# An encoder layer on one core: combinations made in two parts, first weights in a place of their own, v's transposes and the first scores moved back

## The chip, the cores and the metric

The kernel runs on one core of a Trainium2 chip. The metric is the device time of one execution in microseconds (us). The engines are named as the profile names them: PE (TensorE, the matrix engine; PEld are its weight loads), DVE (VectorE), ACT (ScalarE), POOL (GpSimd) and SP (SyncE, which here only issues DMAs). A granted clock of 1.00 means TensorE at full speed.

## The reference

One inference step of a single encoder layer over 576 rows: 512 rows of a new stream (the prompt) and 64 rows of a running stream (the sample), which brings states and 256 past keys and values.

```python
h = layer_norm(ALPHA * x + 0.5 * swiglu_ffn(x, p['ffn1_w_gu'], p['ffn1_w_down']), p['ln1_g'], p['ln1_b'])
mix, new_state = token_mixer(h, p, conv_prev, ml_state, att_past)
h = layer_norm(ALPHA * h + mix, p['ln2_g'], p['ln2_b'])
h = layer_norm(ALPHA * h + 0.5 * swiglu_ffn(h, p['ffn2_w_gu'], p['ffn2_w_down']), p['ln3_g'], p['ln3_b'])
```

```python
def token_mixer(xn, p, conv_prev, ml_state, att_past):
    (ml_q, ml_k, ml_v, ml_o, ml_i, ml_f, a_q, a_k, a_v, g_ml, g_att) = jnp.split(xn @ p['w_in'], SPLIT_IDX, axis=-1)
    ...
    qk = jax.nn.silu(causal_dwconv(qk_pad, p['ml_conv_w'], p['ml_conv_b']))
    ...
    h_ml, (C1, n1, m1) = mlstm_run(qm, km, vm, li, lf, (C0.astype(f32), n0.astype(f32), m0.astype(f32)))
    ...
    y_att = o.reshape(b, t, ATT_WIDTH) @ p['w_att_proj']
    merged = jax.nn.sigmoid(g_ml) * y_ml + jax.nn.sigmoid(g_att) * y_att
    return merged @ p['w_out'], new_state
```

The width is 1024, the FFN's 2816; the mLSTM has 4 heads of 256, the attention 16 heads of 64 with a bias by distance and a causal band in chunks of 64 rows. The sample rows attend to 256 past and 64 new rows. Everything is float32.

## The kernel before

**Arithmetic.** Activations lie transposed, 128 features by 576 rows, in 8 tiles. Each operand of a large product is split into a rounded part ("hi", a cast by ACT) and the rest ("lo", a subtraction by DVE, or by ACT and an accumulating DMA of POOL's queue in `add_lo`). One product is three matmuls: hi·hi, hi·lo, lo·hi (`mm3`, and the inner part of `gemm`). A column tile is 128 output features; its 576 rows go through PE as two halves, in two PSUM banks.

**Order.** PE's order is written out by the program. Class `Order` keeps a virtual clock, `od.now`, to which each matmul adds its estimated nanoseconds; `later(dt, fn)` puts a task into PE's stream once `dt` units have gone by. All the other engines are ordered by a scheduler, by priority (`hot(n)` raises it) and by when an instruction could start; `tc.issue_after(x)` forces an instruction behind x. DMA queues run in the order of their issues: one that waits for its place holds the ones behind it. PSUM has two tags of four banks, "mm" and "aux".

**Weights.** `pump` loads column weights in a fixed plan (`wr`, two buffers), casts and splits them into `wh` and `wl` (NWB = 4 slots). Keys in EARLY and EARLY1 are loaded and split in places of their own (`eh`, `el`) by `early`, long before use; keys in ADDED take their lo part by `add_lo`.

**Pairs.** FFN gate and up columns, and the mLSTM's v and o columns, are made in pairs by a scheme with seven products in place of eight: class `Units` (`prep` parts "a", "s", "t", "u", "b" make the weights' combinations in `ws` and `wt` and split them; `load` brings a pair's raw weights, `wu`, through SP) and class `Combos`. `Combos.add` makes eight sums of activations, `Combos.make` casts and splits them: for t2 and t4 first, then for t1 and t3, all in one go on ACT.

**Stages.** FFN1: first columns by `gemm` (three with WAVE3), then pairs, then the down projection and LN1. Mixer: v, k, q of the first attention pair of heads and the mLSTM gates by one `gemm` in WAVE_M order (so 4 column groups share the PSUM banks), then two v columns from EARLY1, then pairs of v and o columns, whose results go to DRAM (VD, OD). Then eight attention stages `att_qkv(j)`, `att_core(j)`, each for two heads: the transposes of v (`v_tr`), the split and doubled keys kh and kl (`dup`, on POOL, ACT and DVE), the bias tile G with a masked corner written by POOL at the end, and scores (`score`, `score_s`), whose result leaves its bank by a DVE instruction that adds G. The first pair's columns were made in the mixer's first gemm, so in its stage the next pair's columns are the only products around. Then four mLSTM heads: `ml_kq(h)` makes two k and two q columns with their convolutions on DVE and ACT and transposes k (`turn5`); `ml_early(h)` transposes v, whose tiles were loaded from VD in `ml_kq`. Then projections, LN2, and FFN2: four columns by `gemm` in WAVE4 order, whose weights lie in EARLY, then pairs; LN3.

**Places touched.** `Combos.make` and its callers; `Units.load` and the pools `sw` and `cw` for raw weights and sums, `sx` and `cx` for the rest; EARLY and ADDED; `values_s`, which multiplies the sample rows' probabilities (psh, psl) by values vc, where hi and lo of a head stand side by side as 128 columns, so that one matmul makes both, and the halves are added by ACT and DVE afterwards; the start time `t` of the scores in `att_core`; `ml_kq` and `ml_early`.

## Time and profile before

| | us |
|---|---|
| median of 3 runs | 1604.13 (1602.84 to 1610.17) |
| the profiled execution | 1607.91 |
| its span | 1606.1 |
| PE busy | 1576.4 |
| DVE busy | 1051.4 |
| ACT busy | 897.6 |
| POOL busy | 188.0 |

The granted clock over the whole span is 0.994. The span runs from the first to the last instruction. Busy times are summed over an engine's instructions and don't count waits; a row of the list of waits gives the line and tile of the instruction that waited, then what released it, then the total wait, how often, and the longest. Rows of a timeline give the start, the length, the engine, the line, the result's and the operands' names and shapes, and in brackets how long the engine had been idle before it and what ended that.

### The profile page before, as it was taken

Reading aid. Unit: us, or ns where it says so; the run is one execution under the profiler, and the core shown is the slowest. Engines: PE = TensorE matmul, PEld = TensorE weight load, DVE = VectorE, ACT = ScalarE, POOL = GpSimd, SP = SyncE. Lnnn points to the kernel's source line nnn. Section 1 sums busy time; section 2 is a strip of 40 time slices with the busy share of each in tenths; the row PEclk is TensorE's granted clock in tenths of the full one; section 3 lists DMA queues with packets and bytes.
Section 4 is the critical chain, followed back from the end, with each engine's and each line's share of the span. In section 5 each row is a group of like instructions: output and inputs, shape, how many; then the busy total and the mean of one; then the engine's idle time right before and its main releaser. Section 6 shows DMA issues by size and latency. Waiting matters only on the chain. (4 is left out here: it accounts for less than half of the span.)

```text
span 1606.1 us, 29438 instructions
## 1 busy us (share of the span) xinstructions
PE 1576.4 (98%) x11719; PEld 1554.9 (97%) x11719; DVE 1051.4 (65%) x2143; ACT 897.6 (56%) x1624; POOL 188.0 (12%) x349
## 2 busy tenths in 40 slices
PE   9999999999899899999999999999999999999998
PEld 8999999999899899999999999999999999999997
DVE  7777777627756667767623677755677777776636
ACT  7554555324845767767754887683446454555223
POOL 2000000000200432432111121101111000000000
PEclk9999999999999999999999999999999999999999
DMA  9222222224833666666788556533445222213333
GB/s 266 91 105 80 105 80 73 83 86 156 189 125 126 169 147 156 151 148 139 182 200 207 138 125 142 119 101 131 128 109 138 79 106 80 105 54 96 112 90 125
DMA packets 71970, 202.36 MB, mean 126 GB/s; under 512 B 7960, under 2 KB 17816, under 8 KB 71832
## 3 DMA queue, kind: packets, MB, share of 16 engines
q1 hardware_dynamic: 58584, 159.31, 30.3%
q0 software_dynamic: 12672, 40.64, 15.3%
q8 instruction: 92, 1.51, 0.4%
q10 hardware_dynamic: 576, 0.52, 0.1%
q14 instruction: 46, 0.38, 0.1%
HBM read 177.05 MB, written 16.32 MB: 120 GB/s over the span
## 5 line engine op out<-in xcount | busy, mean ns | idle before, releaser
L128 PE MATMUL mm<-s,wh 128*128 128x288 f32 (+2 forms) x3574 | 732.6, 299 | 0.2 <-ACT s L427 0.2
L128 PEld LDWEIGHTS mm<-s,wh 128*128 128x128 f32 x3574 | 576.3, 190 | 3.7 <-issue 0.6
L128 PE MATMUL mm<-s,wl 128*128 128x288 f32 (+2 forms) x1771 | 524.9, 296 | 0.7 <-DVE wl L145 0.7
L128 PEld LDWEIGHTS mm<-s,wl 128*128 128x128 f32 x1771 | 335.8, 190 | 1.0 <-DVE wl L145 1.0
L142 ACT ACTIVATE wh<-wr 128x1024 fp32r<-128x1024 f32 (+2 forms) x147 | 148.1, 1009 | 247.1 <-PE mm L128 224.5
L145 DVE TENSOR_TENSOR wl<-wr,wh 128x1024 fp32r<-128x1024 f32 (+2 forms) x88 | 101.4, 1155 | 102.4 <-ACT wh L142 102.3
L145 DVE TENSOR_TENSOR wl<-ws,wh 128x1024 fp32r<-128x1024 f32 x46 | 56.4, 1225 | 122.3 <-ACT wh L142 122.0
L128 PE MATMUL mm<-h,wh 128*128 128x256 f32 (+1 forms) x672 | 134.7, 294 | 0.0
L142 ACT ACTIVATE wh<-ws 128x1024 fp32r<-128x1024 f32 x46 | 48.8, 1061 | 108.9 <-PE mm L128 107.5
L128 PEld LDWEIGHTS mm<-h,wh 128*128 128x128 f32 x672 | 107.6, 188 | 0.2
L128 PE MATMUL mm<-tx,wh 128*128 128x288 f32 x522 | 106.9, 296 | 0.0
L128 PE MATMUL mm<-h,wl 128*128 128x256 f32 (+1 forms) x336 | 98.7, 294 | 0.0
L450 POOL TENSOR_TENSOR rs<-var,mhalf 128x2 f32<-128x2 f32 (+1 forms) x6 | 5.2, 860 | 737.5 <-DVE var L148 737.5
L128 PEld LDWEIGHTS mm<-tx,wh 128*128 128x128 f32 x522 | 83.4, 188 | 0.0
L182 POOL DMA_DIRECT2D wl<-in_w_in x50 | 45.0, 900 | 280.7 <-ACT wl L142 246.7
L128 PE MATMUL mm<-tx,wl 128*128 128x288 f32 x261 | 76.9, 295 | 0.0
L128 PE MATMUL mm<-tx,ah 128*128 128x288 f32 x344 | 72.2, 302 | 0.1
L142 ACT ACTIVATE wh<-wu 128x1024 fp32r<-128x1024 f32 x46 | 48.9, 1063 | 32.1 <-PE mm L128 31.3
L128 PEld LDWEIGHTS mm<-h,wl 128*128 128x128 f32 x336 | 63.0, 188 | 0.0
L142 ACT ACTIVATE wl<-wh 128x1024 fp32r<-128x1024 f32 x58 | 61.2, 1055 | 0.5
L145 DVE TENSOR_TENSOR ws<-wu 128x1024 f32<-128x1024 f32 x46 | 56.0, 1218 | 7.1 <-DMA wu<-in_w_gu 6.9
L145 DVE TENSOR_TENSOR wl<-wt,wh 128x1024 fp32r<-128x1024 f32 x46 | 56.0, 1218 | 6.5 <-ACT wh L142 6.5
(339 smaller groups left out, 3499.5 us busy)
## 6 DMA issues: line engine op xcount, KB each, us to landing
wu<-in_w_gu SPq DMA_DIRECT2D x78, 512.0 KB, 4.3
wr<-in_w_in SPq DMA_DIRECT2D x58, 512.0 KB, 4.6
wl<-in_w_in POOLq DMA_DIRECT2D x50, 512.0 KB, 5.7
wr<-in_w_dn SPq DMA_DIRECT2D x40, 512.0 KB, 3.6
wr<-in_w_dn SPq DMA_DIRECT2D x20, 384.0 KB, 3.2
wu<-in_w_in SPq DMA_DIRECT2D x14, 512.0 KB, 4.7
G<-in_rbias SPq DMA_DIRECT2D x16, 256.0 KB, 2.9
wr<-in_w_ap SPq DMA_DIRECT2D x8, 512.0 KB, 4.2
```

What stands on the lines that cost most here:

```text
L128: PE.matmul(out, lhsT, rhs, start=start, stop=stop, **kw)
L142: ACT.activation(out, in_, func, **kw)
L145: return (eng or DVE).tensor_tensor(out, a, b, op=op)
L182: POOL.dma_start(lo, src, accum_op=ALU.add)
L450: return y, POOL.tensor_tensor(y, v, mhalf[:, :n], op=ALU.pow)
```

## The change

It has six parts. (1) `Combos.make` casts the sums for t2 and t4, then calls `middle`, which makes the first pair's "a" weights, forced behind the last of these casts; the sums for t1 and t3 are forced behind that. In the mixer, `middle` is forced behind the copy of the second half of q too. (2) The pool for the pairs' raw weights is opened earlier: in FFN2 ahead of the four first columns and in the mixer, where it was open already, its loads are issued ahead of the first gemm; in FFN1 after the first gemm as before; the tile `wt` moves from that pool to the other. (3) The key ("gu2", 1, 1) leaves EARLY; its weights come by `pump`, with `add_lo`. (4) The transposes of v leave `ml_early` and stand in `ml_kq`, 6500 and 13500 units after the k columns; the loads stay. (5) `values_s` makes 18 matmuls with 64 weight columns, summed in PSUM, and two copies, in place of 12 matmuls with 128, a copy and two additions. (6) The first attention pair's scores start at 8500 units in place of 4500.

```diff
-        | {("ap", j) for j in range(KT)}
-
-    EARLY = [("gu2", j, e) for j in range(2) for e in range(2)]
+        | {("ap", j) for j in range(KT)} | {("gu2", 1, 1)}
+
+    EARLY = [("gu2", 0, 0), ("gu2", 0, 1), ("gu2", 1, 0)]
...
-        def make(self):
+        def make(self, middle):
...
+            after = None
             for n, (ka, kb) in ((1, ("t2", "t4")), (0, ("t1", "t3"))):
                 for i in range(4):
                     t, hi, lo = self.sums[2 * i + n], self.tile(), self.tile()
-                    act(hi, t)
-                    add_lo(lo, hi, t)
+                    with tc.issue_after(after.ins) if after is not None else nullcontext():
+                        last = ACT.activation(hi, t, AF.Copy)
+                        add_lo(lo, hi, t)
...
+                if n:
+                    with tc.issue_after(last.ins):
+                        after = middle()
...
-                r = self.wp.tile([P, 2, 512], F32, tag="wt", name=nm("wt"), bufs=1)
+                r = self.pool.tile([P, 2, 512], F32, tag="wt", name=nm("wt"), bufs=1)
...
+            def weights():
+                un.wp = wstack.enter_context(tc.tile_pool(name=nm("sw"), bufs=1, side="right", reuse_waits="tile"))
+                un.load(j0)
+                un.load(j0 + 1)
...
             if prev is None:
...
                 gemm([key(0, 0), key(0, 1), key(1, 0)], xs, [gate_cb(0), up_cb(0), gate_cb(1)], WAVE3,
                      ["mm", "mm", "aux"])
+                weights()
             else:
+                weights()
                 gemm([key(0, 0), key(0, 1), key(1, 0), key(1, 1)], xs, [gate_cb(0), up_cb(0), gate_cb(1), up_cb(1)], WAVE4)
...
-                un.load(j0)
-                un.load(j0 + 1)
-                combos.make()
-                un.prep(j0, "a")
+                combos.make(lambda: un.prep(j0, "a"))
...
         def values_s(th, tl):
             po = bank()
-            blocks = (P, 5), (P, 6), (NS, 4)
             for e in range(2):
                 r = slice(64 * e, 64 * e + 64)
-                for b, (ks, vb) in enumerate(blocks):
-                    for x in (th, tl):
-                        mm(po[:, r], vc[:ks, vb, e, :], x[:ks, b, r], b == 0 and x is th, b == 2 and x is tl)
-            tmp = ap_.tile([P, P], F32, tag="ts", name=nm("ts"))[0:64, :]
-            act(tmp, po[64:128, 0:P])
+                for b, (ks, vb) in enumerate(((P, 5), (P, 6), (NS, 4))):
+                    mm3(po[0:64, r], vc[:ks, vb, e, 0:64], vc[:ks, vb, e, 64:128], th[:ks, b, r], tl[:ks, b, r],
+                        b == 0, b == 2)
             for e in range(2):
-                r = slice(64 * e, 64 * e + 64)
-                tt(o_[r, NP_:T], po[0:64, r], tmp[:, r], ALU.add)
-
-        t = 4500
+                act(o_[64 * e:64 * e + 64, NP_:T], po[0:64, 64 * e:64 * e + 64])
+
+        t = 4500 if j else 8500
...
+    un.load(0)
+    un.load(1)
     for i, key in enumerate(EARLY1):
         later(9000 + 4000 * i, lambda key=key: early(e1, key, EARLY1))
     gemm([[(("in", 48), KT)], [(("in", 40), KT)], [(("in", 32), KT)], [("if", KT)]], H,
-         [out_cb(vf0, "v", 0), out_cb(kf0, "k", 0), lambda hf, ps: act(hs(qf0, hf), ps), gate_cb], WAVE_M)
+         [out_cb(vf0, "v", 0), out_cb(kf0, "k", 0), q0_cb, gate_cb], WAVE_M)
...
-        combos.make()
-        un.prep(0, "a")
+        def middle():
+            with tc.issue_after(q0[1].ins):
+                return un.prep(0, "a")
+        combos.make(middle)
...
         for e in range(2):
-            v = slot(F32, mp, "vf", bufs=2)
-            SP.dma_start(v, VD[2 * h + e])
-            st["v"].append(v)
+            vf = slot(F32, mp, "vf", bufs=2)
+            SP.dma_start(vf, VD[2 * h + e])
             SP.dma_start(st["og"][e], OD[2 * h + e])
+            ce = slice(e * P, (e + 1) * P)
+            def v_sink(b0, nb, w, v4, ce=ce):
+                act(vh[:w, b0:b0 + nb, ce], v4)
+                tt(vl[:w, b0:b0 + nb, ce], v4, f(vh[:w, b0:b0 + nb, ce]), ALU.subtract)
+            later(6500 + 7000 * e, lambda vf=vf, s=v_sink: turn5(vf, s))
...
     def ml_early(h, st):
         st["W"] = W = []
-        for e, vf in enumerate(st["v"]):
-            ce = slice(e * P, (e + 1) * P)
-            def v_sink(b0, nb, w, v4, ce=ce):
-                act(vh[:w, b0:b0 + nb, ce], v4)
-                tt(vl[:w, b0:b0 + nb, ce], v4, f(vh[:w, b0:b0 + nb, ce]), ALU.subtract)
-            later(1000 + 1300 * e, lambda vf=vf, s=v_sink: turn5(vf, s))
```

More of the change, by code (lines that the diff above doesn't have):

```diff
@@ L710, in parts @@
                 hi, lo = (wpool.tile([P, 1024], F32R, tag=t, name=nm(t), bufs=NWB) for t in ("wh", "wl"))
-            act(hi, src)
+            self.last = ACT.activation(hi, src, AF.Copy)
             tt(lo, src, f(hi), ALU.subtract)
@@ L736, in prep @@
                 del self.raw[j]
+            return getattr(self, "last", None)
         def product(self, ps, j, wk, xk, start, last):
@@ L892, in ffn @@
         with tc.tile_pool(name=nm("hr"), bufs=FT, side="right", reuse_waits="tile") as hr, \
-                tc.tile_pool(name=nm("h0"), bufs=2 * NH0, side="right", reuse_waits="tile") as h0:
+                tc.tile_pool(name=nm("h0"), bufs=2 * NH0, side="right", reuse_waits="tile") as h0, ExitStack() as wstack:
             def gate_cb(j):
@@ L909, in ffn @@
             combos = Combos(xs, raw, [hr.tile([P, T], F32, tag="h", name=nm("h"), bufs=FT + 1) for _ in range(8)])
+            j0 = CL[n]
+            un = GateUp(n, j0, hr, None, None, combos)
+            def weights():
+                un.wp = wstack.enter_context(tc.tile_pool(name=nm("sw"), bufs=1, side="right", reuse_waits="tile"))
+                un.load(j0)
+                un.load(j0 + 1)
             if prev is None:
@@ L921, in ffn @@
                 prev.close()
-            with tc.tile_pool(name=nm("sw"), bufs=1, side="right", reuse_waits="tile") as sw, \
-                    tc.tile_pool(name=nm("sx"), bufs=1, side="right", reuse_waits="tile") as sx:
-                combos.pool = sx
-                un = GateUp(n, CL[n], hr, sx, sw, combos)
+            with wstack, tc.tile_pool(name=nm("sx"), bufs=1, side="right", reuse_waits="tile") as sx:
+                combos.pool = un.pool = sx
                 hp_ = Hidden(hh, [(h0, "h0", 2 * NH0), None, None, (hr, "h", FT + 1)])
@@ L935, in ffn @@
                 un.hr_done = hr_done
-                j0 = CL[n]
-                un.load(j0)
-                un.load(j0 + 1)
-                combos.make()
-                un.prep(j0, "a")
+                combos.make(lambda: un.prep(j0, "a"))
                 rest = [(1, 1)] if prev is None else [(2, 0), (2, 1)]
@@ L1263, in att_core, with q0_cb @@
                 t += 1500
+    q0 = []
+    def q0_cb(hf, ps):
+        q0.append(ACT.activation(hs(qf0, hf), ps, AF.Copy))
     pstack = ExitStack()
@@ L1269, in tile_layer, with keep_v, keep_o @@
     combos = Combos(H, ln1.d, [slot(F32, stp, "st", bufs=8) for _ in range(8)])
+    VD, OD = [away("vd") for _ in range(KT)], [away("od") for _ in range(KT)]
+    def keep_v(c, tiles):
+        for e in range(2):
+            SP.dma_start(VD[c + e], tiles[e])
+    def keep_o(c, tiles):
+        for e in range(2):
+            act(tiles[e], tiles[e], AF.Sigmoid)
+            SP.dma_start(OD[c + e], tiles[e])
+    pairs = [(c, b) for c in range(0, KT, 2) for b in (16, 24)][1:]
+    un = Columns([(b + c, b + c + 1) for c, b in pairs],
+                 [lambda tiles, c=c, fn=keep_v if b == 16 else keep_o: fn(c, tiles) for c, b in pairs],
+                 stp, None, cw, combos)
+    un.load(0)
+    un.load(1)
     for i, key in enumerate(EARLY1):
@@ L1272, in tile_layer @@
     gemm([[(("in", 48), KT)], [(("in", 40), KT)], [(("in", 32), KT)], [("if", KT)]], H,
-         [out_cb(vf0, "v", 0), out_cb(kf0, "k", 0), lambda hf, ps: act(hs(qf0, hf), ps), gate_cb], WAVE_M)
-    VD, OD = [away("vd") for _ in range(KT)], [away("od") for _ in range(KT)]
+         [out_cb(vf0, "v", 0), out_cb(kf0, "k", 0), q0_cb, gate_cb], WAVE_M)
     for i in range(4):
@@ L1280, in tile_layer @@
         combos.pool = cx
-        def keep_v(c, tiles):
-            for e in range(2):
-                SP.dma_start(VD[c + e], tiles[e])
-        def keep_o(c, tiles):
-            for e in range(2):
-                act(tiles[e], tiles[e], AF.Sigmoid)
-                SP.dma_start(OD[c + e], tiles[e])
-        pairs = [(c, b) for c in range(0, KT, 2) for b in (16, 24)][1:]
-        un = Columns([(b + c, b + c + 1) for c, b in pairs],
-                     [lambda tiles, c=c, fn=keep_v if b == 16 else keep_o: fn(c, tiles) for c, b in pairs],
-                     stp, cx, cw, combos)
-        un.load(0)
-        un.load(1)
-        combos.make()
-        un.prep(0, "a")
+        un.pool = cx
+        def middle():
+            with tc.issue_after(q0[1].ins):
+                return un.prep(0, "a")
+        combos.make(middle)
         for c in range(2):
@@ L1450, in ml_kq @@
     def ml_kq(h):
-        st = {"k": [], "q": [], "og": [slot(F32, hp, "og") for _ in range(2)], "v": []}
+        st = {"k": [], "q": [], "og": [slot(F32, hp, "og") for _ in range(2)]}
         kwh = mp.tile([P, 5, 256], F32R, tag="kwh", name=nm("kwh"))
```

## The prediction

> **What bounds the kernel now.** I read the head of the page first, then TensorE's list of waits, then windows around the longest of them, and last the single instructions that end them.

> ```profile
> span 1606.1 us, 29438 instructions
> PE 1576.4 (98%) x11719; PEld 1554.9 (97%) x11719; DVE 1051.4 (65%) x2143; ACT 897.6 (56%) x1624; POOL 188.0 (12%) x349
> ```

> TensorE (PE) is busy 98% of the span. The other engines have much to spare on average, so time can go only where PE waits or runs at a lower clock, or where its own instructions change. Its waits, by line waiting and tile waited for (total, times, longest):

> ```profile
> PE mm L128 <- ACT vf L142: 3.7, 1, 3.7
> PE aux L138 <- DVE vl L145: 3.2, 3, 1.1
> PE aux L128 <- DVE wl L145: 3.1, 2, 1.9
> PE aux L138 <- ACT s L142: 2.7, 1, 2.7
> PE aux L128 <- DVE kl L1127: 1.4, 1, 1.4
> PE aux L128 <- POOL kh L152: 1.2, 1, 1.2
> PE aux L138 <- ACT Mb L142: 1.0, 1, 1.0
> ```

> These are the waits at the edited places: 3.7 at the mixer's first columns, 2.7, 1.4 and 1.2 at the first attention pair, 3.2 and 1.0 at the mLSTM's transposes of v, 3.1 at the pairs' first weights in the two FFNs. They sum to 16.3 us, the scale of the whole case. What they cost beyond themselves is in the windows (stretch, its length, busy us of PE, PEld, DVE, ACT, POOL with counts, granted clock, DMA share, GB/s):

> ```profile
> 404.80:409.60 4.80, 4.80 (x29) 4.72 (x28) 3.10 (x6) 3.41 (x5) 3.22 (x4) 0.65 0.86 298
> 429.00:433.20 4.20, 0.57 (x4) 0.31 (x3) 1.96 (x4) 4.17 (x9) 3.37 (x5) 1.00 1.07 185
> 433.20:437.00 3.80, 3.72 (x18) 3.72 (x19) 1.57 (x2) 3.75 (x10) 1.33 (x2) 0.55 1.08 194
> 526.00:541.00 15.00, 11.03 (x82) 10.32 (x80) 8.14 (x19) 10.05 (x17) 8.58 (x17) 1.00 0.76 216
> 541.00:556.00 15.00, 13.20 (x78) 12.71 (x79) 11.52 (x49) 10.70 (x31) 5.99 (x12) 0.77 0.55 143
> 542.30:549.20 6.90, 6.39 (x31) 6.12 (x32) 5.55 (x26) 4.28 (x13) 1.07 (x2) 0.53 0.74 182
> 866.00:887.00 21.00, 21.00 (x161) 20.98 (x159) 14.48 (x26) 14.29 (x28) 4.04 (x13) 1.00 0.79 177
> 887.00:895.00 8.00, 6.95 (x52) 6.33 (x52) 7.01 (x18) 7.95 (x20) 1.59 (x6) 1.00 0.81 199
> ```

> After the mixer's wait and after the scores' waits the clock is near a half (0.55 and 0.53): a wait is paid twice there. After the transposes of v it is not (1.00).

> **Mixer: the order in `make`.** ScalarE (ACT) and PE before:

> ```profile
> 423.90 0.69 ACT L142 ACTIVATE tx<-st 128x576 fp32r<-128x576 f32 x1 [0.97 <-DVE st L148]
> 432.79 0.44 ACT L142 ACTIVATE vf<-mm 128x320 f32<-128x320 f32 x1
> 427.80 1.78 PE L128 MATMUL mm<-s,wh 128*128 128x320 f32 x11
> 433.28 0.59 PE L128 MATMUL mm<-s,eh 128*128 128x256 f32 x2 [3.71 <-ACT vf L142]
> ```

> PE stops at 427.80 + 1.78 = 429.58: its next product needs a bank that vf's second half still holds, and that copy stands on ACT behind the casts and lower parts of all eight sums, begun at 423.90. Idle: 4.20 − 0.57 = 3.63. Then 3.72 us of work at 0.55 of the clock, 1.67 over its full-speed time. Together 5.3. The diff makes the second half of these casts wait for prep "a", and prep "a" for the last copy of q. So ACT does the first half, (432.79 − 423.90) / 2 = 4.4 us, until 428.3, then vf, kf and qf, and only then prep's cast and the other half. The copy comes some 4 us sooner, PE does not stop, and the half clock, which follows the stop, goes too: −5.3. The moved casts also move four accumulating DMAs on POOL's queue; the sums they feed are used after two more columns, and ACT falls behind by one copy group and one cast, under 3 us. Bounds: −5.3, and −4.3 if the gate columns' copies, now nearer the casts, cost 1 us.

> **First attention pair: scores 4000 later.**

> ```profile
> 533.62 0.45 DVE L1127 CAST kl<-kl 64x576 fp32r<-64x576 f32 x1
> 538.66 0.15 POOL L1080 MEMSET G<- 64x64 f32 x1
> 538.84 0.29 DVE L1177 CUSTOM_DVE_ANT_0 sc<-aux,G 128x128 f32<-128x128 f32 x1 [2.77 <-POOL G L1080]
> ```

> Idle PE in 526 to 541: 3.97; in 541 to 556: 1.80; at 0.53 of the clock, 6.39 us of work lose 3.0. Together 8.8. Cause: the scores stand in PE's order before kh and kl exist, columns of the next tile stand behind them, and a finished column's copy queues on ACT behind exponentials (the 2.7). kl is ready at 533.62 + 0.45 = 534.07 and ends the wait of 1.4; with the 1.2 before it, and some 0.3 of score between, PE first stood at 531.2. 4000 units of the order's clock are 4 us of PE's own work, and columns are there to fill it: the first score comes at 535.2, 1.1 after kl. The waits of 1.2 and 1.4 go. What is late next is the bias tile G: POOL comes to it last and finishes it at 538.81; VectorE (DVE) waited 2.77 for it. The first score's bank comes free at 538.84 + 0.29 = 539.1. Of the four banks of this kind the values' and transposes' results hold some, so I let the third score wait for it: by the diff's steps it stands 900 + 1100 units after the first, at 537.2, and waits 1.9. So −8.8 + 1.9 = −6.9. Bounds: −8.8 if there is a bank, −5.0 if a lower clock doubles the 1.9.

> Does it double? Rows here say both: after the wait of 3.7 the clock was 0.55, and in 404.8 to 409.6 it was 0.65, where no wait of this list lies; after 1.0 at the transposes it stayed 1.00. I take no doubling, nearest to the 1.0. [...]

> The pair's own tiles are single: kh and kl of the second pair can be written only when the first pair's scores are done. A shift of 4 on the first pair takes 4 us of the second's cover; as the second's scores don't wait in the list of before, I put nothing.

> **The mLSTM's transposes of v: behind the k columns.**

> ```profile
> L138 PE MATMUL aux<-ident,vf 128*128 128x128 f32 (+1 forms) x40 | 6.4, 275 | 4.3 <-DVE vl L145 3.2 <-ACT Mb L142 1.0
> L138 PE MATMUL aux<-ident,qf 128*128 128x128 f32 (+1 forms) x40 | 5.8, 276 | 0.0
> vf<-vd SPq DMA_DIRECT2D x8, 288.0 KB, 3.0
> ```

> The transposes of v wait 4.3 us in four heads, since both of a head come together in the stretch like 887 to 895, where ACT is busy 7.95 of 8.00 and DVE 7.01. The k and q columns stand in stretches like 866 to 887, where PE is never idle, the transposes of k and q wait 0.0, and DVE is busy 14.48 and ACT 14.29 of 21. The move carries at most the 7.0 and 7.95 us of the old place into 6.5 and 6.7 free ones, and in truth only the sinks' part of it: −4.3. SyncE's loads of vf stay where they are issued and land in 3.0, while the transposes come 6500 units after. Bounds −4.3 to 0 (and see the last rival).

> **Pairs' first weights in the FFNs.**

> ```profile
> SPq L703 <- PE mm L128: 31.3, 1, 31.3
> 1225.35 7.01 DMA wu<-in_w_gu
> 1241.89 1.15 DVE wl L145
> 1243.09 1.58 PE aux L128 x10
> 36.21 1.06 ACT L142 ACTIVATE wh<-wu 128x1024 fp32r<-128x1024 f32 x1
> ```

> In FFN2 the loads stand at the head of SyncE's queue for 31.3 us for their place, then take 7.01, and DVE comes to the last lower part only at 1241.89 to 1243.04, 1.9 after PE wanted it. With a place of their own they can start before FFN2's first columns, over 7.01 sooner, where 1.9 is wanted: −1.9. What queues behind them on SyncE is the later columns' weights; those, and prep's cast, which still needs a cast buffer that PE frees late, make the upper bound +1. The one weight tile that leaves EARLY for the ordinary pump is loaded and split during LN2's stage; its cast and lower part need no longer than the 7.01 of a load, and the stage in which it waits is longer: nothing. In FFN1 the wait's other 1.2 is set by ACT, which casts without a break until 36.21 + 1.06; a new order shifts work on it and takes none away: −0.4, bounds −2 to +0.5.

> **Decode-row values as 64-column products.**

> ```profile
> 588.92 0.20 PE L128 MATMUL aux<-psh,vc 128*128 128x64 f32 x1
> 589.17 0.28 PE L128 MATMUL aux<-psl,vc 128*128 128x64 f32 x1
> 589.38 0.29 PE L128 MATMUL aux<-psh,vc 64*128 64x64 f32 x1
> 590.62 0.55 PE L138 MATMUL aux<-ident,sc 128*128 128x128 f32 x3
> 577.24 0.19 PE L128 MATMUL aux<-kh,qs 128*64 128x64 f32 x1
> 577.33 0.31 PE L128 MATMUL aux<-kh,qs 128*64 128x256 f32 x1
> 577.62 0.22 PE L128 MATMUL aux<-kl,qs 128*64 128x64 f32 x1
> 577.90 0.33 PE L138 MATMUL aux<-ident,sc 128*128 128x128 f32 x1
> ```

> Twelve products take 590.62 − 588.92 = 1.70 now, 0.142 each. The new form has 18 of 64 columns. In the score of the same rows two such take 577.33 − 577.24, 0.045 each; a change of column width costs 577.90 − 577.62 less 0.045 = 0.23, one of row height 589.38 − 589.17 less 0.045 = 0.16. Four of these and one width: 18 × 0.045 + 4 × 0.16 + 0.23 = 1.68. So 0 over eight pairs. Bounds: with no dear change 18 × 0.045 = 0.81, −7.1 in all; at 0.142 each 2.55, +6.8. [...] DVE loses two additions and ACT gains one copy, beside PE's columns: nothing.

> **Sum.** −5.3 − 6.9 − 4.3 − 1.9 − 0.4 + 0 = −18.8. The profiled execution took 1607.91, its span 1606.1, the rest lies around it; the median of the three runs, 1604.13, is 3.8 below it. 1607.91 − 18.8 = 1589.1, and against the median 1585.3: I say 1585. With every part at its better end (−5.3, −8.8, −4.3, −1.9, −2, −7.1) it would be 1604.1 − 29.4 = 1575; at its worse (−4.3, −5.0, 0, +1, +0.5, +6.8) 1603.

> **Rivals.** (a) The scores' waits only change their names: G at 538.81 stays, and every score after the fourth stands behind it, with the half clock after it, so the 6.9 is not won: 1604.1 − 11.9 = 1592. For: DVE's 2.77 for G. Against: the later scores leave 4 us less to wait. (b) The casts stay ahead of vf on ACT, because the order was only partly forced: the mixer's 5.3 stays, 1590.5. Against: the edit adds explicit orders. (c) The values are dearer, +6.8: 1592; the row of 0.045 speaks against it. [...] (d) The changes do not reach the path at all, since each stall is set by something that stays: 1604. Against: five separate places would have to fail. (e) Slower: a head's two v turns now meet k's and q's convolutions on DVE and ACT; their banks come free late and PE, all busy there today, stops at each of the eight. Without the 4.3, 14.5 is left; it is used up at 14.5 / 8 = 1.8 us a turn, and from (14.5 + 8) / 8 = 2.8 a turn the kernel is slower by over 0.5%. The worst wait of the list, 3.7 a turn, gives 1604.1 − 14.5 + 29.6 = 1619. For: DVE and ACT are over two thirds busy there. Against: the same kind of turns of k and q wait 0.0 there.

> **How the numbers follow.** The forecast has 0.62 (own range 1580 to 1590), (a) 0.12, (b) 0.08, (c) 0.06, (d) 0.04, (e) 0.08. The range reaches from the forecast's better end past (a), (b) and (c): 1577 to 1597; (d), (e) and the tails are outside. Half a per cent, 8 us, is about what a measurement here tells from no change: 1596 is the bound. Forecast, (a), (b), (c) lie below it, 0.88, less 0.02 for two of them at once: faster 0.86. (d) and the mild part of those and of (e): same 0.07. The rest of (e), slower 0.07.

> **What would show it.** Right: no wait of PE for vf near 433, and clock 1.00 there; the first score near 535 with no wait for kh or kl and a short one for G's users; ident,vf with no idle time; wu's loads over 7 us ahead of the old 1225; the values in 1.6 to 1.8. Wrong: PE waits for vh or vl in the k and q stretches (e); the half clock after 537 (a); all the casts still ahead of vf's copy (b); 2.5 us a set of values (c).

## The result and the profile after

The changed kernel takes 1614.14 us (median of 10, 1609.14 to 1619.99), the kernel before 1606.57 in the same series (median of 10): a ratio of 1.0052, 95% interval 1.0035 to 1.0070. It is slower by about 7.6 us; forecast were 1585 and 19 us less. The head of the page after, and TensorE's waits in it (line and tile waiting, released by, total us, times, longest):

```profile
span 1612.5 us, 29503 instructions
PE 1577.7 (98%) x11767; PEld 1554.0 (96%) x11767; DVE 1047.4 (65%) x2127; ACT 895.4 (56%) x1630; POOL 187.4 (12%) x349
```

```profile
PE aux L138 <- DVE psl L145: 4.3, 1, 4.3
PE aux L128 <- DVE mx L1188: 3.1, 2, 2.3
PE aux L138 <- DVE og L148: 3.0, 5, 1.1
PE mm L128 <- ACT hb L887: 3.0, 2, 1.8
PE mm L128 <- ACT h L142: 2.5, 1, 2.5
PE aux L138 <- DVE kwl L148: 2.0, 2, 1.7
PE mm L128 <- DVE hb L145: 1.9, 2, 1.0
PE aux L128 <- DVE wl L145: 1.9, 1, 1.9
PE aux L128 <- DVE vl L145: 1.5, 3, 0.6
PE mm L128 <- DVE s L145: 1.4, 2, 1.2
```

Of the waits that the prediction listed only wl and vl are still there, and at other places. Others have come or grown: psl and mx in the first attention pair (mx was 0.8 and 0.4 before), og, kwl and vl in the mLSTM, h and wl in FFN1, s ahead of FFN2, and hb, which the prediction never named.

Where the time went can be read off closely, because both kernels send the same 9892 products into the "mm" banks in the same order. The start of the i-th of them in one timeline, less its start in the other, is the delay gathered so far; its growth over a stage is what the stage lost or won. For example the mixer's first product with early weights starts at 433.28 before and here at 436.40, 3.1 later, where for the product just ahead of it the delay had been 7.0:

```profile
436.40 0.40 PE L128 MATMUL mm<-s,eh 128*128 128x256 f32 x2
```

The growth by stage, in us against the profile of before (worked out so from each kernel's trace; minus is won):

```
stage                        forecast  after  a_wt a_t4500 a_vold a_make1 a_fix  b_wt   b_v
FFN1, first columns            -0.4     4.8    4.1    4.5    4.8   -0.6   -0.3   -0.9  -1.4
FFN1, first hidden tiles         -      3.6    0.0    4.4    4.4    4.2    0.0    2.7   0.0
LN1                              -     -1.4   -1.5   -1.4   -1.4   -1.4   -1.6   -1.5  -1.7
mixer, first columns           -5.3    -5.5   -5.5   -5.5   -5.5   -5.5   -5.5    0.6   0.0
first attention pair           -6.9     0.9    0.9   -0.4    1.3    2.3    0.2   -2.2  -1.7
six further pairs               0.0    -1.6   -1.5   -1.5   -1.5   -1.5   -1.5   -0.1  -0.1
mLSTM heads                    -4.3     3.5    5.5    3.5    2.4    5.4   -0.1   -0.1   3.5
LN2 and FFN2's start           -1.9    -2.3   -2.5   -2.4   -2.3   -2.4   -2.5   -3.5   5.0
FFN2, first hidden tiles         -      4.2    0.0    4.2    4.1    2.5    0.0    4.0   0.0
```

The column "after" sums to 6.2; the spans differ by 6.4. LN1's −1.4 is not the change's: b_wt and b_v below, which alter one part elsewhere, show −1.5 and −1.7, and the trace of before has a clock of 0.50 from 406.24 to 409.65, where that of after has 1.00 (404.8 to 409.6). Each column is one execution, so an entry under some 2 us can be such chance (see the end). Three parts did as forecast in sum: the mixer, FFN2's start, and, better than the 0 taken, the values. Four cost time: FFN1's order, wt's place (the hidden tiles), v's transposes and the scores, 17.0 in all.

### The profile page after: what moved, and what is told of

Read it like the earlier page. It is cut to its first block, busy times and chain, and to the rows that moved or that the text cites. A ratio compares the mean times of both kernels' runs of the same rounds, so it can differ in the third digit from the quotient of the medians.

```text
span 1612.5 us, 29503 instructions
## 1 busy us (share of the span) xinstructions
PE 1577.7 (98%) x11767; PEld 1554.0 (96%) x11767; DVE 1047.4 (65%) x2127; ACT 895.4 (56%) x1630; POOL 187.4 (12%) x349
## 5 line engine op out<-in xcount | busy, mean ns | idle before, releaser
L128 PE MATMUL mm<-s,wh 128*128 128x288 f32 (+2 forms) x3606 | 738.9, 298 | 3.0 <-ACT h L142 2.5
L128 PEld LDWEIGHTS mm<-s,wh 128*128 128x128 f32 x3606 | 580.9, 190 | 7.3 <-ACT h L142 2.7
L128 PE MATMUL mm<-s,wl 128*128 128x288 f32 (+2 forms) x1787 | 529.3, 296 | 0.2 <-DVE wl L145 0.2
L128 PEld LDWEIGHTS mm<-s,wl 128*128 128x128 f32 x1787 | 338.6, 189 | 0.4 <-DVE wl L145 0.4
L142 ACT ACTIVATE wh<-wr 128x1024 fp32r<-128x1024 f32 (+2 forms) x148 | 149.0, 1009 | 258.6 <-PE mm L128 233.0
L145 DVE TENSOR_TENSOR wl<-wr,wh 128x1024 fp32r<-128x1024 f32 (+2 forms) x88 | 101.1, 1153 | 108.2 <-ACT wh L142 108.1
L145 DVE TENSOR_TENSOR wl<-ws,wh 128x1024 fp32r<-128x1024 f32 x46 | 56.4, 1226 | 125.5 <-ACT wh L717 125.3
L128 PE MATMUL mm<-h,wh 128*128 128x256 f32 (+1 forms) x672 | 134.7, 294 | 0.0
L128 PEld LDWEIGHTS mm<-h,wh 128*128 128x128 f32 x672 | 107.6, 188 | 0.2
L128 PE MATMUL mm<-tx,wh 128*128 128x288 f32 x522 | 107.5, 297 | 0.0
L128 PE MATMUL mm<-h,wl 128*128 128x256 f32 (+1 forms) x336 | 98.7, 294 | 0.0
L128 PEld LDWEIGHTS mm<-tx,wh 128*128 128x128 f32 x522 | 84.0, 189 | 0.0
L128 PE MATMUL mm<-tx,wl 128*128 128x288 f32 x261 | 77.1, 295 | 0.0
L128 PE MATMUL mm<-tx,ah 128*128 128x288 f32 x344 | 72.3, 302 | 0.1
L145 DVE TENSOR_TENSOR wl<-wt,wh 128x1024 fp32r<-128x1024 f32 x46 | 56.1, 1220 | 12.0 <-ACT wh L717 12.0
L128 PEld LDWEIGHTS mm<-h,wl 128*128 128x128 f32 x336 | 63.0, 188 | 0.0
L128 PE MATMUL mm<-hb,wh 128*128 128x256 f32 (+1 forms) x280 | 58.0, 298 | 4.9 <-ACT hb L887 3.0
L142 ACT ACTIVATE wl<-wh 128x1024 fp32r<-128x1024 f32 x59 | 62.3, 1056 | 0.6
```

What stands on the lines that cost most here:

```text
L128: PE.matmul(out, lhsT, rhs, start=start, stop=stop, **kw)
L142: ACT.activation(out, in_, func, **kw)
L145: return (eng or DVE).tensor_tensor(out, a, b, op=op)
```

## The experiments

Four runs undo one part of the change each, three repair or isolate, two do one part alone, three look for the best mix. "before" is timed beside each; the changed kernel is not, so a difference to it is one of medians from two series, good to some 2.5 us (an estimate: twice the standard error, from the spread of the runs).

**a_wt: the tile wt out of the combinations' pool.**

```diff
-                r = self.pool.tile([P, 2, 512], F32, tag="wt", name=nm("wt"), bufs=1)
+                r = getattr(self, "tp", self.pool).tile([P, 2, 512], F32, tag="wt", name=nm("wt"), bufs=1)
...
-            with wstack, tc.tile_pool(name=nm("sx"), bufs=1, side="right", reuse_waits="tile") as sx:
+            with wstack, tc.tile_pool(name=nm("sv"), bufs=1, side="right", reuse_waits="tile") as sv, \
+                    tc.tile_pool(name=nm("sx"), bufs=1, side="right", reuse_waits="tile") as sx:
+                un.tp = sv
```

> The changed kernel with one thing undone: the tile wt lies in a small pool of its own just behind the pool of raw weights, so that the down projection's first hidden tiles (hb) come to lie over raw weights and sums again and no longer over activations' combinations. Theory (place in memory): in the changed kernel hb's first cast waits until 267.6 because its place is held by a combination that the last pair still reads; with the pool the cast comes near 254, the two waits of PE for hb (1.75 and 0.97 near 268, and the like in FFN2) go, 3.3 in FFN1 and 3.7 in FFN2 are won: 7 us under the changed kernel, about 1607. Rival (order): hb is late because the other engines' order changed with make; then the waits for hb stay and the time is that of the changed kernel, 1614.

Measured: 1607.41, ratio 1.0015 (1.0002 to 1.0028), 6.7 under the changed kernel. The first hidden cast on ACT, before, after, and in this run:

```profile
249.14 0.67 ACT L880 ACTIVATE hb<-h 128x576 fp32r<-128x576 f32 x1
```

```profile
267.60 2.96 ACT L887 ACTIVATE hb<-h 128x576 fp32r<-128x576 f32 x5
```

```profile
253.28 0.67 ACT L887 ACTIVATE hb<-h 128x576 fp32r<-128x576 f32 x1
```

After, PE wants hb at once behind the last pairs' products and stands twice, for the cast and for the lower part:

```profile
268.32 0.39 PE L128 MATMUL mm<-hb,wh 128*128 128x256 f32 x1 [1.75 <-ACT hb L887]
269.68 0.39 PE L128 MATMUL mm<-hb,wh 128*128 128x256 f32 x1 [0.97 <-DVE hb L145]
```

In a_wt neither wait is there, in FFN1 or in FFN2 (3.6 and 4.2 in the table become 0.0). By the sizes in the code, ten hidden tiles of 2304 bytes a partition, 23,040, fit over the pool of raw weights and sums while it holds two raw tiles, ws and wt (24,576); without wt it holds 20,480, and the first hidden tiles reach into the combinations' place, which is read until the last pair is done. That reading fits this run and the next; which tile held the place was not traced.

**b_wt: that line alone, in the kernel before.**

```diff
-                r = self.wp.tile([P, 2, 512], F32, tag="wt", name=nm("wt"), bufs=1)
+                r = self.pool.tile([P, 2, 512], F32, tag="wt", name=nm("wt"), bufs=1)
```

> The kernel before with one line of the change alone: the tile wt comes from the pool of the combinations in place of that of the raw weights. Theory (place in memory): the down projections' first hidden tiles then lie over combinations in both FFNs; the waits for hb come (1.7 and 1.0 in each), 3.3 in FFN1 and 3.7 in FFN2 are lost, 7 in all: 1613. Rival (order): without the change's other edits nothing moves, 1606.

One run: 1607.24, against a median of 1607.89 for before (1603.95 to 1611.47). The waits came, as by the first theory:

```profile
PE mm L128 <- ACT hb L880: 2.1, 2, 1.1
PE mm L128 <- DVE hb L145: 1.9, 2, 1.0
```

By stages the hidden tiles lose 2.7 in FFN1 and 4.0 in FFN2, near the 7 named. But the run is not slower: LN2 and FFN2's start win 3.5, LN1 1.5, the first pair 2.2. Most of that is no doing of the line: LN1, the 1.1 of the 3.5 that fall in LN2, and probably the first pair are what the trace of before had lost by chance. The other 2.2 are the line's: the loads of the pairs' raw weights are issued from 1218.90, where they came at 1224.98 before, and the wait for wl there is gone. So the line alone explains the hb waits, and the expectation left out that the smaller pool of raw weights also gives FFN2's start what I had put down to the early loads. What the line costs in the whole, one run doesn't tell.

**a_make1: FFN1's combinations in one go.**

```diff
-                combos.make(lambda: un.prep(j0, "a"))
+                if prev is None:
+                    combos.make(None)
+                    un.prep(j0, "a")
+                else:
+                    combos.make(lambda: un.prep(j0, "a"))
```

> The changed kernel with FFN1's combinations made in one go again, prep a behind them (FFN2 and the mixer keep the two parts). Theory (order on ACT): in the changed kernel ACT takes prep b's small cast ahead of the rest, waits 0.9 for its weights, and the first columns' copies come 2 us later, and the wait for wl moved from 39.1 to 42.3; with one go the waits of 2.5 near 28 and 1.9 near 42 shrink to those of the kernel before (0.7 and 1.2): 4 us under the changed kernel, 1610. Rival (the load): the copies came late because the raw weights' load landed 1.6 us later in that execution; then FFN1's start differs from run to run with either order and this run is within 1 us of the changed kernel.

Measured: 1609.88, ratio 1.0020 (1.0006 to 1.0033), 4.3 under the changed kernel; FFN1's start goes from +4.8 to −0.6. The column's load did land late in the profile of after (ACT's cast of it starts at 21.02 there), but in a_wt that cast starts at 19.35, and FFN1 still lost 4.1: the order is what counts. The lines of after (timelines of ACT and PE, then windows):

```profile
24.83 0.63 ACT L717 ACTIVATE ah<-wu 128x512 fp32r<-128x512 f32 x1 [0.88 <-DMA wu<-in_w_gu]
27.92 0.38 ACT L142 ACTIVATE h<-mm 128x256 f32<-128x256 f32 x1
28.36 0.50 PE L128 MATMUL mm<-s,wh 128*128 128x256 f32 x2 [2.45 <-ACT h L142]
42.35 0.40 PE L128 MATMUL aux<-s,wl 128*128 128x288 f32 x1 [1.88 <-DVE wl L145]
```

```profile
25.00:28.36 3.36, 0.91 (x8) 0.65 (x6) 2.22 (x4) 3.33 (x6) 0.86 (x1) 1.00 0.73 138
42.00:46.00 4.00, 3.65 (x16) 3.65 (x17) 1.87 (x4) 1.50 (x3) 0.00 (x0) 0.58 0.71 135
```

ACT is full here (3.33 of 3.36). Forcing half of the casts back frees a place that the scheduler gives to prep b's cast ah, which stands on ACT until its weights land; the columns' copies and later the second pair's weights come after it. PE pays 2.45 and 1.88, and runs at 0.58 of the clock afterwards. The 2.45 is large in this execution because of the late load: in a_wt, a_t4500, a_vold, a_dup and a_mask, which have the same order, the wait for h is 0.4 to 1.0. What all five have is a wait of 1.8 for the second pair's wh, one of 1.8 or 1.9 for its wl (1.2 before and in a_make1). In a_wt a clock of 0.50 stands behind them:

```profile
42.00:46.00 4.00, 4.00 (x19) 4.00 (x18) 1.32 (x2) 1.45 (x3) 0.00 (x0) 0.50 0.22 43
```

I did not force ah alone to its old place.

**a_t4500: the first scores back at 4500.**

```diff
-        t = 4500 if j else 8500
+        t = 4500
```

> The changed kernel with the first pair's scores back at 4500. Theory (the move only relocates the stall): the waits of 1.2 and 1.4 for kh and kl and the 2.7 for s come back near 532 to 542, the wait of 4.3 for psl and the half clock behind it go; the stage from 526 to 600 takes within 2 us of what it takes in the changed kernel, so 1612 to 1616. Rival (the prediction): the move had gained 6.9 here and something else ate it; then this run is some 7 us slower than the changed kernel, 1621.

Measured: 1611.76, ratio 1.0027 (1.0012 to 1.0042), 2.4 under the changed kernel. The waits for kh, kl and s are back at 1.2, 1.4 and 2.7, psl's is gone, and the stage goes from +0.9 to −0.4. The 2.4 is not clear of the noise by itself, and the two ratios' intervals overlap; but in all traces with the scores at 8500 and nothing else moved in this stage it stands at +0.9 to +2.3 (the changed kernel, a_wt, a_vold, a_make1), and in all with 4500 at −2.2 to +0.2. After, the stage in windows, and what stands on DVE ahead of psl:

```profile
526.00:541.00 15.00, 13.19 (x104) 12.92 (x102) 7.23 (x12) 12.11 (x19) 6.78 (x13) 1.00 0.84 255
541.00:556.00 15.00, 13.48 (x98) 12.80 (x98) 13.40 (x54) 11.20 (x30) 9.38 (x19) 1.00 0.82 202
556.00:571.00 15.00, 11.79 (x66) 11.45 (x67) 6.68 (x15) 6.77 (x16) 2.79 (x6) 0.66 0.40 96
```

```profile
553.00 1.08 DVE L145 TENSOR_TENSOR kl<-s,kh 64x576 fp32r<-64x576 f32 x1
556.07 0.42 DVE L145 TENSOR_TENSOR psl<-aux,psh 128x256 fp32r<-128x256 f32 x1
556.52 1.05 DVE L145 TENSOR_TENSOR kl<-s,kh 64x576 fp32r<-64x576 f32 x1
558.78 0.28 DVE L145 TENSOR_TENSOR psl<-aux,psh 64x128 fp32r<-64x128 f32 x1
```

The gain is there: PE idles 1.81 from 526 to 541, where it idled 3.97 before, and from 541 to 556 the clock stays at 1.00. It is paid back behind it: DVE is busy 13.40 of 15, the next pair's kl goes ahead of psl and between its two instructions, PE idles 3.21 from 556 to 571 and works at 0.66.

**a_dup: the next pair's dup later too.**

```diff
-            later(640 + 5240 * e, lambda e=e: dup(kf, 0, T, e))
+            later(640 + 5240 * e + (4000 if j == 1 else 0), lambda e=e: dup(kf, 0, T, e))
```

> The changed kernel with one task moved: the split and doubling of the second pair's own keys (dup of kf) starts 4000 units later, as far as the first pair's scores had been moved. Theory (queue order on DVE): in the changed kernel that task's subtractions and casts for kl stand on DVE ahead of psl, which PE needs; with them behind it the wait of 4.3 for psl falls under 1.5 and the half clock from 556 to 571 (0.66) goes, some 6 us less from 526 to 601. Rival (the softmax chain itself is late): psl is late because its own scores were moved 4000; then the wait for psl stays near 4.

One run, 1610.73. The wait for psl goes and one for ptl takes its place:

```profile
PE aux L138 <- DVE ptl L145: 3.1, 1, 3.1
```

The stage goes from +0.9 to −1.3, and the clock from 556 to 571 from 0.66 to 0.89: 2.2 won, not 6. So the queue's order is part of it, and DVE's crowd hands the wait on to the next in line.

**a_mask: G's mask early.**

```diff
-            later(4000, mask)
+            later(4000 if j else 1000, mask)
```

> The changed kernel with the first pair's bias mask written 1000 instead of 4000 units after the loads. Theory (G is late on POOL): the first score leaves its bank at 541.1 because POOL writes G's mask at 540.9, behind the splits of the past keys; with the mask near 537 the wait of PE for mx (2.3 near 541) falls under 0.5. The wait for psl then stays. Rival (the load): G itself lands about 537, 4.6 us after its issue at 531.5 to 532.4, and POOL stands still for it, so the past values and keys get later by as much and the waits only change place: less than 1 us is won from 526 to 601.

One run, 1612.80, and inconclusive: the scheduler moved the mask by one place on POOL only, from 540.94 to 540.00, and the wait for mx from 2.3 to 2.1. Neither theory was put to the test.

**a_vold and b_v: v's transposes.** a_vold puts them back in ml_early; b_v takes them to ml_kq in the kernel before and changes nothing else.

```diff
-            later(6500 + 7000 * e, lambda vf=vf, s=v_sink: turn5(vf, s))
+            st["v"].append(vf)
...
+            later(1000 + 1300 * e, lambda vf=vf, s=v_sink: turn5(vf, s))
```

> The changed kernel with the transposes of v back in ml_early. Theory (sinks crowd DVE and ACT in the k and q columns): the waits for og (3.0), kwl (2.0), vl (1.7) go, the four waits near 1.1 for vl and Mb come back; the four heads get 3 to 4 us shorter, 1610. Rival (the prediction): the heads get 4.3 us longer, 1618; a milder rival: no difference within 1 us, the heads' 3.6 came from elsewhere.

> The kernel before with the transposes of v in ml_kq alone. Theory (sinks crowd DVE and ACT): the four waits near 1.1 go and waits for og, kwl and vl come in their place, by stages 0.6 to 1 us a head lost, 3 in all: 1609. Rival (the prediction): 4.3 won, 1602.

a_vold: 1612.22, ratio 1.0031 (1.0017 to 1.0046); b_v, one run, 1611.47 against a median of 1607.89 (1603.95 to 1611.47). In b_v the four heads lose 3.5 by stages, near the 3 expected, with the waits of the changed kernel to the tenth; the list of b_v from 860 to 1100:

```profile
PE aux L138 <- DVE og L148: 3.0, 5, 1.1
PE aux L138 <- DVE kwl L148: 2.0, 2, 1.7
PE aux L128 <- DVE vl L145: 1.5, 3, 0.6
PE aux L138 <- DVE vl L145: 0.2, 1, 0.2
```

6.7 us stand against 4.2 before (3.2 and 1.0). In a_vold these lines are gone and the old ones back (Mb's at 1.9); three heads are within 0.1 of before, but the first lost 2.4, with a clock of 0.72 from 892 to 896 and 0.85 from 896 to 900 (see the end). Its 1.9 under the changed kernel is not clear of the noise, so here the waits and stages carry the argument, not the totals. One head, after (timeline of PE, then the window):

```profile
938.61 0.76 PE L138 MATMUL aux<-ident,qf 128*128 128x128 f32 x5 [1.12 <-DVE og L148]
```

```profile
924.00:976.00 52.00, 49.73 (x370) 47.67 (x369) 35.72 (x90) 35.60 (x76) 8.47 (x26) 1.00 0.56 129
```

PE idles 2.27 here. The transposes of v wait in one head only any more, the first, 1.7 us for kwl; those of q and of the previous head's output (hf) wait in the others, since their banks are emptied by DVE (og, kwl). That DVE comes to og and kwl late because the sinks of v stand ahead of them fits a_vold and b_v, but was not followed on DVE. b_v also lost 5.0 at LN2 and FFN2's start, with a wait of 2.4 for DVE's s and a clock of 0.77 there; I have no cause for the wait.

**a_fix: the four slow parts undone.** It keeps the mixer's and FFN2's two parts, the early loads and the 64-column values; the edits are those of a_wt, a_t4500, a_vold and a_make1 together.

> The changed kernel with four parts undone: wt in a pool of its own behind the raw weights, FFN1's combinations in one go, scores at 4500, v's transposes in ml_early. What is left of the change: the mixer's and FFN2's combinations in two parts, FFN2's early loads and its one tile out of EARLY, the mixer's early loads, the values as 64-column products. Theory (sum of the single undoings, by starts of the same products in the traces): FFN1 -0.6, hidden tiles 0, LN1 -1.5, mixer -5.5, first pair -0.4, values -1.5, heads 0, LN2 and FFN2 -2.2: -11.7 against the kernel before, 1595. Rival (gains don't add, each stall only hands on to the next or to a half clock): within 4 us of the kernel before, 1603 or more.

Measured: 1596.76 against 1606.20 for before in that series, ratio 0.9934 (0.9913 to 0.9955): faster than both kernels. By stages −11.1 where −11.7 was summed up; 1.6 of it is LN1's, which the profile of before had lost by chance. Among its waits:

```profile
PE aux L138 <- DVE vl L145: 3.2, 3, 1.1
PE mm L128 <- DVE s L145: 1.4, 2, 1.2
```

The parts add within the noise: the four undoings alone won 6.7, 2.4, 1.9 and 4.3, together 15.3; all at once 1614.14 − 1596.76 = 17.4.

**a_fix8, f_t6000, f_vhalf: can the two moves be had?** All three are a_fix with something put back: the scores at 8500 with a_dup's and a_mask's edits; the scores at 6000; only the first of a head's two v turns moved.

```diff
-        t = 4500
+        t = 4500 if j else 6000
```

```diff
+            if e == 0:
+                later(6500, lambda vf=vf, s=v_sink: turn5(vf, s))
+            else:
+                st["v"] = vf, v_sink
...
+        later(1700, lambda vf=st["v"][0], s=st["v"][1]: turn5(vf, s))
```

> As the run before with the scores at 8500 for the first pair, the first mask early and the second pair's dup 4000 later (the two repairs of this call together). Theory: the first pair's stage loses 5 to 7 us less than in the kernel before, so 1589 in all. Rival: the shift of the first pair is worth nothing in any company; then it equals the run before, 1595, or is slower by 1 to 2.

> The run a_fix (1596.8) with the first pair's scores at 6000 in place of 4500. Theory (DVE and ACT are full in this stage, so what PE doesn't wait for kh and kl it waits for later): the waits of 1.2 and 1.4 shrink by 1.5 together, and the stage from 526 to 601 changes by less than 1.5 us; 1595 to 1598. Rival (8500 was only too far): 3 us or more won, 1593.

> The run a_fix (1596.8) with one of a head's two v turns moved: the first goes to ml_kq at 6500, the second stays in ml_early at 1700. Theory (it is the second turn that lands in a crowd): the waits near 1.1 for vl and Mb go since the two turns no longer share banks, and at 6500 the first costs less than 0.5 a head: 2 to 4 us under a_fix, 1594. Rival (any turn among the convolutions costs what it saves): within 1 us of a_fix or slower.

Medians and ratios: 1596.71, 0.9935 (0.9913 to 0.9958); 1597.51, 0.9939 (0.9919 to 0.9960); 1596.92, 0.9931 (0.9909 to 0.9954). None can be told from a_fix. In the traces a_fix8 wins 2.8 in the first pair and loses 2.9 in the first head; f_t6000 wins 1.1 in the first pair; f_vhalf has no wait for Mb and less for vl, but og's is 3.4, and its heads lose 1.1. For a_fix8 and f_vhalf the rival held, for f_t6000 the theory: nothing is won here by moving alone.

## Why the prediction was wrong

**The mixer was right**: −5.5 for −5.3, by its own mechanism. In the windows of before PE worked 0.57 of 4.20 us and then at 0.55. After, the same work stands some 3 to 7 us later, and vf's copy goes ahead of half the casts; PE neither stops nor slows:

```profile
433.38 0.44 ACT L142 ACTIVATE vf<-mm 128x320 f32<-128x320 f32 x1
```

```profile
432.00:436.20 4.20, 4.20 (x31) 4.20 (x30) 4.20 (x10) 4.05 (x9) 2.26 (x3) 1.00 0.74 167
436.20:440.00 3.80, 3.80 (x32) 3.80 (x31) 2.74 (x4) 3.80 (x7) 1.39 (x3) 1.00 1.00 214
```

That before's loss here was no chance is seen in b_wt and b_v, which keep the old order and come to +0.6 and 0.0.

**FFN2's start was right in size, partly by luck**: −2.3 with LN2 for −1.9. The loads start at 1145.94, and PE, busy 6.00 of 6.00, is full where the chain of loads, sums and lower parts had stopped it; that wins 2.2. But b_wt shows the smaller pool alone to give as much, so the early issue, the step by which I got there, is not shown to be the cause. And two things of 1.1 each cancel in the sum: before's wait of 0.9 for s in LN2, which is gone in b_wt as well, and a new wait of 1.2 for s at the first columns, which a_fix has as well and before, b_wt and b_v have not. There a weight column's lower part now stands on DVE among LN2's outputs. I had put the weights that leave EARLY at nothing; that they are the cause fits, but no run undoes that part alone.

```profile
1145.94 1.09 SPq L709 DMA_DIRECT2D wu<-in_w_gu  x2
1210.53 1.21 DVE L145 TENSOR_TENSOR wl<-wr,wh 128x1024 fp32r<-128x1024 f32 x1
1215.29 0.41 PE L128 MATMUL mm<-s,eh 128*128 128x320 f32 x1 [1.20 <-DVE s L145]
```

```profile
1240.00:1246.00 6.00, 6.00 (x46) 6.00 (x45) 5.34 (x7) 2.12 (x3) 0.00 (x0) 1.00 0.94 175
```

**The values were mis-sized, harmlessly**: a set takes 591.65 − 590.20 = 1.45, not 1.68. I had taken 0.045 off the 0.21 ahead of a change of height, but the products around it have 128 weight columns and start 0.11 apart (588.95 to 589.06 in before), so a change costs 0.10, not 0.16. In the new form products start 0.06 apart, and 0.15 where the height changes, also where the width changes with it: 18 × 0.06 + 4 × 0.09 = 1.44. The six further pairs won 1.6, 0.27 each, not 0.

```profile
590.20 0.19 PE L128 MATMUL aux<-psh,vc 128*64 128x64 f32 x1
591.45 0.22 PE L128 MATMUL aux<-psl,vc 64*64 64x64 f32 x1
591.50 0.22 PE L128 MATMUL aux<-psh,vc 64*64 64x64 f32 x1
591.65 0.66 PE L138 MATMUL aux<-ident,sc 128*128 128x128 f32 x4
```

**A term was missing**: +7.8 for the hidden tiles. The prediction has no word on wt's new pool: it followed loads and products, and never asked who comes to lie in a freed place next. In before these casts start at 249.14, 18 us earlier than the 267.60 of after (13.6 if the 4.8 of delay gathered by then is taken off), so nothing in the waits of before pointed to them.

**FFN1, "−0.4, bounds −2 to +0.5"**, came to +4.8, and to 4.1 to 4.8 in the other traces of this order. The step that failed is "a new order shifts work on it and takes none away". On a full engine a forced order also decides what else goes ahead, and that was a cast whose operand had not landed.

**The first pair, −6.9**, came to +0.9. "4000 units are 4 us of PE's own work, and columns are there to fill it" was right for PE: the first score comes at 536.81, with 1.5 of delay gathered before the stage, where 535.2 was put. What was taken as late next, G, was indeed late: the third score's wait for mx is 2.3 where 1.9 was put. The failed step is what is late after that: with the softmax 4 us later and the next pair's keys not, DVE has both at once. I had set the second pair's scores against the shift, not its dup. Rival (a) named the outcome, that the waits only change their names and a half clock follows (0.66 from 556 to 571), but put it down to G; it was psl, 4.3.

**The transposes of v, −4.3**, came to +3.5. The step that failed is the reading of "idle 0.0": the row of qf's transposes showed that nothing waited there with DVE at 14.48 of 21, and I took free time on DVE for a place in its queue. Rival (e) named this mechanism. The waits grew, but by less than its price: 6.7 / 8 = 0.84 us of waits a turn, under the 1.8 at which it alone would have used up the gain. So the sign of the whole came from four parts together, and the chance of 0.07 for it was too low for a sum in which three terms rested on the same kind of step.

## What to carry to other kernels

A wait that one engine ends is not removed by moving its cause in time on that engine's queue; ask which task then stands at its old place, and count the queue's order, not its idle share. A tile that changes its pool also changes what lies over it later: look for the next owner of that memory. Where a change has many parts, single undoings tell more than one sum: here the parts that a_fix keeps were worth 9.4 us (1606.20 to 1596.76), and four others hid them.

## What the runs showed of the hardware that I had not expected

A wait of some 2 us is followed by a lower clock in one execution and not in another, and not by its length. At the first mLSTM head PE waits 1.7 us for kwl in the changed kernel and 2.1 in a_wt; at the first attention pair it waits 2.29 for mx in the changed kernel. The windows there, the changed kernel's and then a_wt's:

```profile
537.56:540.97 3.41, 1.63 (x13) 1.36 (x11) 0.40 (x1) 1.98 (x3) 3.03 (x8) 1.00 0.71 229
540.97:544.39 3.42, 2.92 (x18) 2.83 (x19) 3.20 (x16) 2.24 (x8) 3.04 (x9) 1.00 0.37 94
889.13:892.55 3.42, 1.76 (x14) 1.52 (x14) 2.73 (x8) 3.42 (x11) 0.71 (x5) 1.00 0.85 202
892.55:895.96 3.41, 3.41 (x28) 3.41 (x27) 3.31 (x7) 3.36 (x6) 0.86 (x1) 1.00 0.65 147
```

```profile
885.89:889.30 3.41, 1.36 (x12) 1.36 (x13) 2.73 (x8) 3.41 (x12) 0.72 (x5) 1.00 0.72 203
889.30:892.71 3.41, 3.41 (x18) 3.41 (x17) 2.66 (x7) 3.36 (x4) 0.86 (x1) 0.50 0.56 114
```

The 2.29 costs no clock, the 2.1 costs 3.41 us at 0.50.

The changed kernel's windows are counted in pieces of 3.413 us from 28.98, where its first half clock starts, a_wt's back and on from 889.30, where this one starts. Between 12 and 1585 us the traces of before and after hold seven stretches at half clock, all at 0.50, and each is 3.41, 6.83 or 10.24 us long. In the changed kernel the later three start 13.65, 529.06 and 1430.18 us behind the first, which is 4, 155 and 419 times 3.413. PE's busy time in the 3.41 us ahead of each:

```
kernel  half clock from  for     PE busy in the 3.41 us ahead
before  406.24            3.41   2.89
before  433.54            3.41   0.26
before  542.77            6.83   0.70
after    28.98            3.41   0.97
after    42.63            3.41   1.25
after   558.04           10.24   0.33
after  1459.16            3.41   1.32
```

In 3.41 us at half clock a full PE loses some 3.41 × 0.5 = 1.7 us of its work (an estimate from the clock on record). Between 12 and 1585 us before has 4 such pieces and the changed kernel 6; a_fix has 3 from 526 to 556, worked out from its clock there (0.75 and 0.91, over 15 us each). The first pair, with its scores at 4500 throughout, differs by stages from −2.2 (b_wt) to +0.2 (a_fix). A difference of 2 us in one profile is no evidence here.
